# One decoder layer on one core: sample-state loads issued behind the weights, the prompt read in eight pieces, the first layer norm's output kept as the second residual

## The chip, the cores and the metric

The kernel runs on one core of a Trainium2 chip. The metric is the device time of one execution, in microseconds (us). A core has a matrix engine (PE, with its weight loads listed apart as PEld), a vector engine (DVE), a scalar engine (ACT), a general engine (POOL) and a synchronisation engine (SP); each takes its own instructions strictly in their order. Loads and stores are DMAs: SP, ACT or POOL issues one, 16 DMA engines carry it out, and a semaphore tells when it has landed.

## The reference

One layer for two groups of requests that share all weights: 256 prompt tokens and 8 sample tokens (one for each of 8 requests), model width 2048. Cut to what matters here:

```
proj = x @ w_in                      # 16400 columns: q, k, v, g, a, conv inputs, memory query, gates z_a, z_b, z_m
A: gated linear attention            # per head a 256 x 512 state; S_new = decay * S + k^T v
B: short gated convolution
M: cross-attention into 256 memory tokens
merged = sig(z_a)*y_a + sig(z_b)*y_b + sig(z_m)*y_m
x  = LayerNorm(alpha * x + merged @ w_o)                    # first layer norm
f  = (silu(dwconv3(x @ w_gate)) * (x @ w_up)) @ w_down
x  = LayerNorm(alpha * x + f)                               # second residual: the first norm's output
```

The prompt starts from zero states. Each of the 8 samples brings its own memory keys and values (`cache_mem_k`, `cache_mem_v`, 256 rows each) and, for each of 4 heads, its own state of 256 x 512 numbers (`state_gla`), and the new states are outputs. All arrays are fp32.

## The kernel before

**Matrix products.** All 264 tokens (256 prompt, 8 sample) stand as columns; a weight matrix is streamed once, in *granules* of two k-tiles by 512 columns (512 KB). A granule is loaded by one DMA that SP issues (`ws`, four buffers), rounded to a high part by ACT (`wh`, three buffers) and its remainder is formed by DVE (`wl`, three buffers), lines 238 to 257. PE then runs three products for each of its 8 tiles: wh with the activations' high part, wh with their low part, wl with the high part (lines 279 to 281), so 24 matmuls of 264 columns for a granule. Some 650 granules follow each other: w_in's groups, the memory weights, w_o, then for the feed-forward part a first pass over 24 of 43 column tiles of gate and up with its share of w_down, and a second pass over the other 19. A `group` is 512 output columns: eight granules for a depth of 2048.

**What shares the queues.** Between the granules the samples' work is threaded in as *units*: 16 for the memory keys, 16 for the values, 32 that read a state (`sum_unit`) and, in the feed-forward part, 32 that update it (`update_unit`, lines 778 to 792). An update unit loads a state tile `S` (512 KB, line 782) and a row of v, copied to all partitions (`T<-dv`, 256 KB, line 784); ACT scales the two halves of S (line 790), DVE adds k times v to each (line 791), and two granules later in program order SP issues the store (line 792). The tiles S have three buffers (tag `S4`), so the load for one unit waits for the store of the unit three before it. Units are put in a list (`queue`); `tick`, called once a granule, pops one when `clock[1]` granules have passed (6 in the feed-forward part) and at least three granules of the group are left, and `ahead` traces the loads of the next ones. The program is then ordered by a list scheduler: program order gives the priority, `high_priority(offset)` moves a piece earlier (granule loads by 700 places, casts by 450), and where an instruction's buffer is free in the scheduler's reckoning it may be put ahead of older ones on its engine. `tc.issue_after(i)` adds an edge: instructions traced inside it stand behind instruction i on their engine, without a wait.

**The start.** The prompt x (256 x 2048) comes in four pieces of 512 columns, two DMAs of 256 KB each (`load_x`, line 73); the samples' rows `xs` come by SP. PE keeps busy with nine products of constants (`keep_warm(9)`, line 99), each recorded as two passes, transposes x tile by tile (line 305, 128 x 128) into PSUM, and `split` (line 289) makes the high part XH on ACT and the low part XL on DVE. `turn_start` (line 308) does the samples and the first four k-tiles; `turn_x`, called from the first group's granules, loads the other pieces and transposes two k-tiles a granule.

**The residuals.** `residual` (line 1008) adds a high and a low part on POOL into a tile of tag `T4` (16 buffers). It is called four times on XH, XL for the first layer norm and four times on X1H, X1L, the split output of the first norm, for the second (line 1120). The normalised tile itself (`r`, line 1073) is split and then released.

Of the kernel before, what the change touches and what calls it, by code (L numbers as in the profile page):

```python
# [9 lines left out]
F32 = mybir.dt.float32  # L10
# [7 lines left out]
P = 128  # L18
NP = 256
# [15 lines left out]
def layer_kernel(ctx, tc, x_prompt, x_sample, mem_prompt, cache_mem_k, cache_mem_v, state_gla, state_conv,  # L35
# [3 lines left out]
    nc = tc.nc  # L39
# [11 lines left out]
    def big(dt=F32, shape=(P, 4, NT)):  # L51
        return sb.tile(list(shape), dt, tag="T4", bufs=16, name=nm("T4"))
# [17 lines left out]
    xc = []  # L70
    xs = t2(F32, (P, P))

    def load_x(c):
        t = big(F32, (P, 2, 512))
        for m in range(2):
            (nc.sync if m or c else S).dma_start(t[:, m], x_prompt[0, m * P:(m + 1) * P, c * 512:(c + 1) * 512])
        xc.append(t)

    load_x(0)
    nc.sync.dma_start(xs, x_sample.rearrange("b l (k f) -> (b l k) f", f=P))  # L80

# [16 lines left out]

    keep_warm(9)
    LEVELS = (1, 2, 4, 8, 16, 32, 64)  # L100
# [59 lines left out]
    queue = []  # L160
    loaded = [0]
    clock = [0, 4]
# [6 lines left out]
    def ahead(n):  # L169
        k = 0  # L170
        for it in queue:
            if it[0] is not None:
                it[2] = it[0]()
                it[0] = None
            if it[2] is not None:
                k += 1
            if k >= n:
                break
# [59 lines left out]
    def granule(srcs, n, ncols):  # L238

        lead[0] += 1  # L240
        with tc.high_priority(offset=0 if lead[0] <= 8 else 700):
            st = sb.tile([P, n, ncols], F32, tag="ws", bufs=4, name=nm("ws"))
            for a, o in srcs:
                c = a.shape[-1]
                nc.sync.dma_start(st[:, :, o:o + c], a.rearrange("(k p) c -> p k c", p=P))
        with tc.high_priority(offset=0 if lead[0] <= 8 else 450):
            wh = sb.tile([P, n, ncols], F32R, tag="wh", bufs=3, name=nm("wh"))
            wl = sb.tile([P, n, ncols], F32R, tag="wl", bufs=3, name=nm("wl"))
            with ExitStack() as after:
                if lead[0] == 1:  # L250
                    S.copy(wh, st)
                for i in first.pop(0) if first else []:
                    after.enter_context(tc.issue_after(i))
                if lead[0] > 1:
                    S.copy(wh, st)  # L255
                V.tensor_sub(wl, st, wh.bitcast(F32))  # L256
        return wh, wl
# [36 lines left out]
    def turn_x(g, n):  # L294
        if g in (0, 2, 4):
            load_x(len(xc))
        if g + 4 <= 16 and g:
            for kt in range(g + 2, g + 4):
                with tc.high_priority(offset=60):
                    turn_x1(kt)  # L300

    def turn_x1(kt):
        pt = small()
        for m in range(2):
            T.transpose(pt[:, m * P:(m + 1) * P], xc[kt // 4][:, m, kt % 4 * P:(kt % 4 + 1) * P], ident)
        return split(XH[:, kt, 0:NP], XL[:, kt, 0:NP], pt[:, 0:NP])

    def turn_start():
        pt = small()
        T.transpose(pt[:, 0:P], xs, ident)  # L310
        i = split(XH[:, :, NP:NT], XL[:, :, NP:NT], pt[:, 0:P].rearrange("p (b k) -> p k b", b=NS))
        first.append(i + turn_x1(0))
        first.append(turn_x1(1))
        turn_x1(2)
        turn_x1(3)

# [12 lines left out]
    for c in range(2):  # L329
        pm = group([(win, MQ0 + c * 512, 512)], 16, xh, xl, before=None if c else turn_x)  # L330
        t = big()
# [759 lines left out]
    for t0, t1 in ((0, 24), (24, 43)):  # L1091
# [26 lines left out]
        for c in range(4):  # L1118
            if t0 == 0:
                r2.append(residual(c, X1H, X1L))  # L1120
            elif c == 0:
# [114 lines left out]
```

## Time and profile before

| | |
|---|---|
| time, median of 3 runs | 2073.56 us (2070.11 to 2074.78) |
| profiled execution | 2072.68 us, span 2070.7 us |
| mean granted clock of PE | 0.992 |
| PE busy | 2015.7 us (97%) |
| DVE, ACT, POOL busy | 1273.2, 1012.3, 197.1 us |
| DMA | 439.96 MB, mean 212 GB/s |

The profile is that of one execution. A row of a time line or of a group gives start, duration, engine, line and operation, with output<-input; in brackets stands how long the engine had been idle before and what released it. A row of stretches gives the busy time of each engine, with the number of instructions in parentheses, then the clock that PE was granted (1.00 is full, 0.50 half), the DMA engines' mean busy share and GB/s.

### The profile page before, as it was taken

The page shows a single profiled execution, that of the slowest core. Times are in us where ns is not written, and L with a number is a line of the kernel's source. Part 1 is how long each engine was busy: PE and PEld are TensorE (multiplying, and loading weights), DVE is VectorE, ACT ScalarE, POOL GpSimd, SP SyncE. Part 2 cuts the span into 40 slices and gives each one's busy share as a digit, 9 for nine tenths or more (in the row PEclk, how much of TensorE's full clock was granted, in tenths as well). Part 3 has the DMA queues.
Part 4 walks back from the last instruction along what each step waited for, and adds up shares of the span by engine and source line. Part 5 has one row for each costly group of instructions (what it writes and reads, how often), then busy time and mean ns, then how long its engine had stood idle before and what let it go on. Part 6 is the DMA issues. An engine that isn't in the chain of part 4 may idle for free.

```text
span 2070.7 us, 38389 instructions
## 1 busy us (share of the span) xinstructions
PE 2015.7 (97%) x15762; PEld 1965.8 (95%) x15762; DVE 1273.2 (61%) x1902; ACT 1012.3 (49%) x1399; POOL 197.1 (10%) x249
## 2 busy tenths in 40 slices
PE   8999999999999999999999999999899999999996
PEld 8888999999999999999999997988899999999996
DVE  4666585758596755455445769666565445555546
ACT  4433564657474554345444447555454334444432
POOL 4000031303130010100001004000000000000001
PEclk9999999999999999999999999999999999999998
DMA  8796776666577685666565567988896566665753
GB/s 283 237 318 196 230 218 200 210 194 215 179 216 215 197 224 174 180 183 181 179 180 177 177 200 272 312 293 272 296 298 208 179 183 178 180 183 166 234 176 102
DMA packets 233487, 439.96 MB, mean 212 GB/s; under 512 B 22665, under 2 KB 27230, under 8 KB 233048
## 3 DMA queue, kind: packets, MB, share of 16 engines
q1 hardware_dynamic: 227152, 425.42, 66.6%
q0 software_dynamic: 5440, 10.79, 1.6%
q8 instruction: 123, 2.02, 0.4%
q10 hardware_dynamic: 720, 1.31, 0.2%
q14 instruction: 52, 0.43, 0.1%
HBM read 410.76 MB, written 26.85 MB: 211 GB/s over the span
## 4 chain that ended last, share of the span: by engine, by line
PE 60%; DMA 6%; DVE 4%; ACT 1%; issue 1%; SPq 0%; DVEq 0%; ACTq 0%
PE mm L279 19%; PE mm L280 19%; PE mm L281 19%; DMA S<-in_state_gla_dram 5%; DVE wl L256 2%; DMA out_dram<-S 1%; PE sm L725 1%; ACT wh L255 1%; DVE S L791 1%; ACT S L790 0%; DMA T<-dv 0%; PE acc L413 0%; PE acc L414 0%; DVE YT L1195 0%; DVE YT L1201 0%
## 5 line engine op out<-in xcount | busy, mean ns | idle before, releaser
L256 DVE TENSOR_TENSOR wl<-ws,wh 128x1024 fp32r<-128x1024 f32 (+1 forms) x650 | 801.2, 1236 | 587.3 <-ACT wh L255 585.0
L255 ACT CAST wh<-ws 128x1024 fp32r<-128x1024 f32 (+1 forms) x649 | 672.2, 1039 | 794.2 <-PE mm L280 676.4
L279 PE MATMUL mm<-XH,wh 128*128 128x264 f32 (+1 forms) x2064 | 593.1, 287 | 0.2 <-ACT T L814 0.2
L281 PE MATMUL mm<-XH,wl 128*128 128x264 f32 (+1 forms) x2064 | 589.0, 285 | 0.0
L280 PE MATMUL mm<-XL,wh 128*128 128x264 f32 (+1 forms) x2064 | 588.7, 285 | 0.0
L279 PE MATMUL mm<-T,wh 128*128 128x264 f32 x1456 | 415.2, 285 | 0.6 <-ACT G L843 0.6
L281 PE MATMUL mm<-T,wl 128*128 128x264 f32 x1456 | 414.2, 284 | 0.0
L280 PE MATMUL mm<-T,wh 128*128 128x264 f32 x1456 | 414.0, 284 | 0.0
L281 PE MATMUL mm<-X1H,wl 128*128 128x264 f32 x1376 | 394.6, 287 | 13.1 <-DVE wl L256 13.1
L279 PE MATMUL mm<-X1H,wh 128*128 128x264 f32 x1376 | 395.8, 288 | 10.0 <-DVE G L1110 4.6
L280 PE MATMUL mm<-X1L,wh 128*128 128x264 f32 x1376 | 393.1, 286 | 0.5 <-DVE X1L L289 0.5
L279 PEld LDWEIGHTS mm<-XH,wh 128*128 128x128 f32 (+1 forms) x2064 | 389.8, 189 | 2.9 <-ACT T L814 0.4
L280 PEld LDWEIGHTS mm<-XL,wh 128*128 128x128 f32 (+1 forms) x2064 | 389.1, 189 | 2.4
L281 PEld LDWEIGHTS mm<-XH,wl 128*128 128x128 f32 (+1 forms) x2064 | 388.2, 188 | 0.3
L281 PEld LDWEIGHTS mm<-X1H,wl 128*128 128x128 f32 x1376 | 260.4, 189 | 16.5 <-DVE wl L256 16.5
L279 PEld LDWEIGHTS mm<-T,wh 128*128 128x128 f32 x1456 | 274.1, 188 | 1.1 <-ACT G L843 1.1
L279 PEld LDWEIGHTS mm<-X1H,wh 128*128 128x128 f32 x1376 | 261.4, 190 | 13.7 <-DVE G L1110 5.7
L280 PEld LDWEIGHTS mm<-T,wh 128*128 128x128 f32 x1456 | 274.1, 188 | 0.0
L281 PEld LDWEIGHTS mm<-T,wl 128*128 128x128 f32 x1456 | 273.8, 188 | 0.0
L280 PEld LDWEIGHTS mm<-X1L,wh 128*128 128x128 f32 x1376 | 261.1, 190 | 1.2 <-DVE X1L L289 0.7
L791 DVE SCALAR_TENSOR_TENSOR S<-T,qks,S 128x512 f32<-128x512 f32 x64 | 52.9, 851 | 71.0 <-ACT S L790 58.8
L790 ACT ACTIVATE S<-S,eas 128x512 f32<-128x512 f32 x64 | 44.0, 717 | 95.6 <-DMA S<-in_state_gla_dram 95.6
(347 smaller groups left out, 1524.9 us busy)
## 6 DMA issues: line engine op xcount, KB each, us to landing
ws<-in_w_in_dram SPq DMA_DIRECT2D x256, 512.0 KB, 3.7
ws<-in_w_ffn_down_dram SPq DMA_DIRECT2D x84, 512.0 KB, 4.4
ws<-in_w_ffn_gate_dram SPq DMA_DIRECT2D x80, 512.0 KB, 4.3
ws<-in_w_ffn_up_dram SPq DMA_DIRECT2D x80, 512.0 KB, 4.8
S<-in_state_gla_dram SPq DMA_DIRECT2D x64, 512.0 KB, 5.2
ws<-in_w_gla_out_dram SPq DMA_DIRECT2D x32, 512.0 KB, 3.7
ws<-in_w_o_dram SPq DMA_DIRECT2D x32, 512.0 KB, 4.0
out_dram<-S SPq DMA_DIRECT2D x32, 512.0 KB, 7.0
```

Source lines behind the costliest of these rows:

```text
L255: S.copy(wh, st)
L256: V.tensor_sub(wl, st, wh.bitcast(F32))
L279: T.matmul(p, wh[:, t, cs], xh(kt), start=(kt == 0), stop=False)
L280: T.matmul(p, wh[:, t, cs], xl(kt), start=False, stop=False)
L281: T.matmul(p, wl[:, t, cs], xh(kt), start=False, stop=(kt == nk - 1))
L725: T.matmul(pt, kd[:, st, kt * P:(kt + 1) * P], vt[:, st], start=(st == 0), stop=(st == 1))
L790: S.activation(sg[:, kt], sg[:, kt], AF.Copy, scale=eas[:, h, kt, b:b + 1])
L791: V.scalar_tensor_tensor(sg[:, kt], pb, qks[:, 1, h, kt, b:b + 1], sg[:, kt], ALU.mult, ALU.add)
```

## The change

Three edits, and what goes with them.

1. **Loads behind the weights.** `granule` notes its DMA in `staged`; `ahead` traces every unit's loads inside `tc.issue_after(staged[0])`, so that on SP they stand behind the granule last traced.
2. **x in eight pieces.** `load_x` takes 256 columns, two DMAs of 128 KB, 16 in all. The first group's first granule is a single k-tile (g0=1, 256 KB), so that the group has nine granules. Each piece is turned by four transposes into one PSUM tile and one `split` of 512 columns. Through `first`, a granule's cast and remainder are put behind the split of the piece that the granule before it called for. `xs` is loaded by ACT's queue, and `keep_warm` runs 12 products.
3. **Second residual.** `r2` takes the normalised tiles `rs[c]` themselves; the four POOL additions on X1H, X1L go.

```diff
     def load_x(c):
-        t = big(F32, (P, 2, 512))
+        if c % 2 == 0:
+            xc.append(big(F32, (P, 2, 512)))
         for m in range(2):
-            (nc.sync if m or c else S).dma_start(t[:, m], x_prompt[0, m * P:(m + 1) * P, c * 512:(c + 1) * 512])
-        xc.append(t)
+            (nc.sync if m or c else S).dma_start(xc[c // 2][:, m, c % 2 * 256:c % 2 * 256 + 256],
+                                                 x_prompt[0, m * P:(m + 1) * P, c * 256:(c + 1) * 256])
     load_x(0)
-    nc.sync.dma_start(xs, x_sample.rearrange("b l (k f) -> (b l k) f", f=P))
+    S.dma_start(xs, x_sample.rearrange("b l (k f) -> (b l k) f", f=P))
...
-    keep_warm(9)
+    keep_warm(12)
...
         for it in queue:
             if it[0] is not None:
-                it[2] = it[0]()
+                with ExitStack() as behind:
+                    if staged:
+                        behind.enter_context(tc.issue_after(staged[0]))
+                    it[2] = it[0]()
                 it[0] = None
...
-                nc.sync.dma_start(st[:, :, o:o + c], a.rearrange("(k p) c -> p k c", p=P))
+                staged[:] = [nc.sync.dma_start(st[:, :, o:o + c], a.rearrange("(k p) c -> p k c", p=P)).ins]
...
             with ExitStack() as after:
-                if lead[0] == 1:
-                    S.copy(wh, st)
                 for i in first.pop(0) if first else []:
                     after.enter_context(tc.issue_after(i))
-                if lead[0] > 1:
-                    S.copy(wh, st)
+                S.copy(wh, st)
                 V.tensor_sub(wl, st, wh.bitcast(F32))
...
     def turn_x(g, n):
-        if g in (0, 2, 4):
-            load_x(len(xc))
-        if g + 4 <= 16 and g:
-            for kt in range(g + 2, g + 4):
-                with tc.high_priority(offset=60):
-                    turn_x1(kt)
+        c = (g + 1) // 2 + 1
+        if c < 8:
+            load_x(c)
+            with tc.high_priority(offset=60):
+                first.append(turn_x2(c))
+    def turn_x2(c):
+        pt = small()
+        for a in range(2):
+            for m in range(2):
+                T.transpose(pt[:, (2 * a + m) * P:(2 * a + m + 1) * P],
+                            xc[c // 2][:, m, (c % 2 * 2 + a) * P:(c % 2 * 2 + a + 1) * P], ident)
+        return split(XH[:, 2 * c:2 * c + 2, 0:NP], XL[:, 2 * c:2 * c + 2, 0:NP], pt.rearrange("p (a t) -> p a t", a=2))
     def turn_start():
+        first.append(turn_x2(0))
         pt = small()
         T.transpose(pt[:, 0:P], xs, ident)
         i = split(XH[:, :, NP:NT], XL[:, :, NP:NT], pt[:, 0:P].rearrange("p (b k) -> p k b", b=NS))
-        first.append(i + turn_x1(0))
-        first.append(turn_x1(1))
-        turn_x1(2)
-        turn_x1(3)
+        first[0] = first[0] + i
...
-        pm = group([(win, MQ0 + c * 512, 512)], 16, xh, xl, before=None if c else turn_x)
+        pm = group([(win, MQ0 + c * 512, 512)], 16, xh, xl, before=None if c else turn_x, g0=1 - c)
...
             if t0 == 0:
-                r2.append(residual(c, X1H, X1L))
+                r2.append(rs[c])
```

How the instructions move is seen in the order in which they stand on an engine. First SP in the feed-forward part's first pass, at a gate group and the up group behind it; `ws` is a granule, `S` a unit's state, `T<-dv` its row of v, `out_dram<-S` its store. Before:

```order
L245 DMA ws_16039<-in_w_ffn_gate_dram 128x2x512
L792 DMA out_dram<-S_2381_17086 128x2x512
L245 DMA ws_16069<-in_w_ffn_gate_dram 128x2x512
L784 DMA T_2455_17710<-dv 128x512
L782 DMA S_2454_17708<-in_state_gla_dram 128x2x512
L245 DMA ws_16100<-in_w_ffn_gate_dram 128x2x512
L245 DMA ws_16130<-in_w_ffn_gate_dram 128x2x512
L792 DMA out_dram<-S_2410_17339 128x2x512
L245 DMA ws_16194<-in_w_ffn_up_dram 128x2x512
L784 DMA T_2489_17999<-dv 128x512
L782 DMA S_2488_17997<-in_state_gla_dram 128x2x512
L245 DMA ws_16224<-in_w_ffn_up_dram 128x2x512
```

And now:

```order
L784 DMA S_2249_15998<-in_state_gla_dram 128x2x512
L250 DMA ws_16002<-in_w_ffn_gate_dram 128x2x512
L786 DMA T_2250_16000<-dv 128x512
L250 DMA ws_16032<-in_w_ffn_gate_dram 128x2x512
L250 DMA ws_16063<-in_w_ffn_gate_dram 128x2x512
L250 DMA ws_16093<-in_w_ffn_gate_dram 128x2x512
L794 DMA out_dram<-S_2249_15998 128x2x512
L250 DMA ws_16123<-in_w_ffn_gate_dram 128x2x512
L250 DMA ws_16187<-in_w_ffn_up_dram 128x2x512
L784 DMA S_2275_16221<-in_state_gla_dram 128x2x512
L250 DMA ws_16225<-in_w_ffn_up_dram 128x2x512
L786 DMA T_2276_16223<-dv 128x512
```

Before, a unit came every three granules, and a state's load stood one granule behind the store of the unit three before it, whose buffer it takes. Now a unit comes every six granules on average, its own store is issued before the next unit's load, and the buffer that a load takes was stored from some 13 to 15 granules ago. Counted over the whole order, the loads of the 32 update units stood behind granules 392 to 474 and now stand behind 393 to 557 (the first seven still behind 393 to 407); the ACT work on a state stands about two granules ahead of the granule behind which its load is issued, in both.

Second, SP at the start of the program, before (`T` is a piece of x or, 128x128, the samples' rows):

```order
L76 DMA T_2_64<-in_x_prompt_dram 128x512
L80 DMA T_1_63<-in_x_sample_dram 128x128
L245 DMA ws_128<-in_w_in_dram 128x2x512
L76 DMA T_15_134<-in_x_prompt_dram 128x512 x2
L245 DMA ws_161<-in_w_in_dram 128x2x512
L76 DMA T_19_167<-in_x_prompt_dram 128x512 x2
L245 DMA ws_204<-in_w_in_dram 128x2x512
```

And now:

```order
L78 DMA T_2_64<-in_x_prompt_dram 128x256 x2
L250 DMA ws_118<-in_w_in_dram 128x512
L78 DMA T_2_64<-in_x_prompt_dram 128x256
L250 DMA ws_145<-in_w_in_dram 128x2x512
L78 DMA T_16_151<-in_x_prompt_dram 128x256 x3
L250 DMA ws_185<-in_w_in_dram 128x2x512
L78 DMA T_16_151<-in_x_prompt_dram 128x256
L250 DMA ws_224<-in_w_in_dram 128x2x512
L78 DMA T_25_230<-in_x_prompt_dram 128x256 x4
```

Half as much x and half as much weight now stand ahead of the first product, and the fourth granule's weights stand ahead of the fifth piece of x (the first two of the four DMAs into T_25).

Third, PE at the start (`sm<-ident,T` are transposes of x or, 128x128 alone ahead of them, of the samples). Before:

```order
L310 MATMUL sm_98<-ident,T_1_63 128x128
L305 MATMUL sm_102<-ident,T_2_64 128x128 x2
L305 MATMUL sm_107<-ident,T_2_64 128x128 x2
L279 MATMUL mm_124<-XH,wh_130 128x264
L279 MATMUL mm_125<-XH,wh_130 128x264
L305 MATMUL sm_112<-ident,T_2_64 128x128 x2
L280 MATMUL mm_124<-XL,wh_130 128x264
```

And now, from the first transpose and, in the second fence, at the end of the first granule (wh_120, wl_121) and the beginning of the second (wh_147):

```order
L308 MATMUL sm_101<-ident,T_2_64 128x128 x4
L315 MATMUL sm_108<-ident,T_1_63 128x128
L281 MATMUL mm_114<-XH,wh_120 128x264
L308 MATMUL sm_126<-ident,T_2_64 128x128 x4
L308 MATMUL sm_154<-ident,T_16_151 128x128 x4
L282 MATMUL mm_114<-XL,wh_120 128x264
```

```order
L308 MATMUL sm_193<-ident,T_16_151 128x128 x4
L281 MATMUL mm_117<-XH,wh_120 128x264
L282 MATMUL mm_117<-XL,wh_120 128x264
L308 MATMUL sm_233<-ident,T_25_230 128x128 x4
L283 MATMUL mm_117<-XH,wl_121 128x264
L281 MATMUL mm_114<-XH,wh_147 128x264
```

T_2 holds pieces 0 and 1, T_16 pieces 2 and 3, T_25 pieces 4 and 5. Before, the transposes within the first granule's first half were those of the first of four pieces; now the transposes of five of eight pieces, twenty and the samples' one, stand ahead of the first granule's twelfth and last matmul.

More of the change, by code (lines that the diff above doesn't have):

```diff
@@ L160, in layer_kernel @@
     queue = []
-    loaded = [0]
+    staged = []
     clock = [0, 4]
@@ L294, in turn_x @@
     def turn_x(g, n):
-        if g in (0, 2, 4):
-            load_x(len(xc))
-        if g + 4 <= 16 and g:
-            for kt in range(g + 2, g + 4):
-                with tc.high_priority(offset=60):
-                    turn_x1(kt)
-    def turn_x1(kt):
-        pt = small()
-        for m in range(2):
-            T.transpose(pt[:, m * P:(m + 1) * P], xc[kt // 4][:, m, kt % 4 * P:(kt % 4 + 1) * P], ident)
-        return split(XH[:, kt, 0:NP], XL[:, kt, 0:NP], pt[:, 0:NP])
+        c = (g + 1) // 2 + 1
[4 more added lines that the diff above has]
+    def turn_x2(c):
+        pt = small()
+        for a in range(2):
[3 more added lines that the diff above has]
+        return split(XH[:, 2 * c:2 * c + 2, 0:NP], XL[:, 2 * c:2 * c + 2, 0:NP], pt.rearrange("p (a t) -> p a t", a=2))
     def turn_start():
+        first.append(turn_x2(0))
         pt = small()
```

## The prediction

> **What bounds the kernel now.** I read the page's totals first, then the busy time by stretches, then the waits inside the stretch that loses most, then the chain that ended last.
>
> ```profile
> span 2070.7 us, 38389 instructions
> PE 2015.7 (97%) x15762; PEld 1965.8 (95%) x15762; DVE 1273.2 (61%) x1902; ACT 1012.3 (49%) x1399; POOL 197.1 (10%) x249
> ```
>
> PE is the bound: no edit here takes a matmul of 264 columns away, so only its lost time can be won. The stretches say where that lies (columns: PE, PEld, DVE, ACT, POOL, granted clock, DMA share, GB/s).
>
> ```profile
> 1.00:8.00 7.00, 4.59 (x21) 4.23 (x21) 0.56 (x6) 2.68 (x5) 6.07 (x14) 1.00 0.83 234
> 8.70:12.00 3.30, 3.30 (x17) 3.27 (x16) 1.50 (x3) 0.98 (x2) 2.22 (x7) 0.50 1.05 383
> 15.50:18.80 3.30, 2.85 (x13) 2.86 (x14) 2.19 (x4) 1.57 (x3) 3.30 (x10) 0.50 0.92 310
> 1281.90:1285.10 3.20, 2.82 (x13) 2.83 (x14) 3.20 (x3) 1.61 (x4) 2.80 (x1) 0.50 0.81 253
> 1418.40:1421.70 3.30, 3.30 (x14) 3.21 (x15) 3.30 (x6) 2.55 (x6) 0.00 (x0) 0.50 0.60 179
> 1462.80:1466.00 3.20, 3.20 (x16) 3.20 (x16) 1.58 (x2) 0.00 (x0) 0.00 (x0) 0.50 0.87 248
> 1277.00:1553.00 276.00, 252.49 (x1971) 245.54 (x1971) 182.15 (x277) 151.30 (x227) 6.02 (x3) 0.98 0.88 288
> 1560.00:2050.00 490.00, 490.00 (x4030) 489.90 (x4029) 256.02 (x352) 207.29 (x259) 4.93 (x4) 1.00 0.60 180
> 2050.00:2070.70 20.70, 2.87 (x19) 2.04 (x17) 16.53 (x31) 3.70 (x8) 8.46 (x6) 0.66 0.28 105
> ```
>
> From 1560 to 2050 PE never idles and starts a matmul every 490 / 4029 = 0.1216 us; a granule of 24 is then 2.92 us. From 1277 to 1553 it starts only 1971 in 276 us, which at that rate take 239.7: **36.3 us are lost** there, 23.5 as idle time (276 - 252.5), 5.1 in three stretches of about 3.4 us at half clock (half of each), the rest as late weight loads. This stretch holds all 32 state updates. The first 20 us and the tail of 20 us are the other losses; the tail's code is untouched. Who waits in the lossy stretch (line, what it waited for, us in total, times, longest):
>
> ```profile
> ACT S L790 <- DMA S<-in_state_gla_dram: 95.6, 27, 6.3
> DVE S L791 <- ACT S L790: 58.8, 16, 5.4
> DVE wl L256 <- ACT wh L255: 17.9, 14, 5.6
> PE mm L281 <- DVE wl L256: 13.1, 16, 3.2
> PE mm L279 <- DVE G L1110: 4.6, 4, 2.5
> ```
>
> Read from below: PE waits for the weights' remainder or for a bank that DVE empties, DVE for ACT, and ACT stands 95.6 us on 27 states that have not landed, with the casts of later granules queued behind. The chain shows why a state is late:
>
> ```profile
> 1403.10 7.22 DMA out_dram<-S
> 1410.33 6.06 DMA S<-in_state_gla_dram
> 1416.48 0.73 ACT S L790
> ...
> 1417.90 0.42 DVE G L1110
> ```
>
> The load starts the moment a store has landed: the tile's buffer is the stored one. Landing times in this crowd (count, KB, us):
>
> ```profile
> out_dram<-S SPq DMA_DIRECT2D x28, 512.0 KB, 7.1
> S<-in_state_gla_dram SPq DMA_DIRECT2D x27, 512.0 KB, 5.6
> T<-dv SPq DMA_DIRECT2D x19, 256.0 KB, 7.3
> ```
>
> A store and the load behind it need 7.1 + 5.6 = 12.7 us, against three granules (8.8 us) from one unit to the next.
>
> **The loads behind the weights.** SP's order now has a unit every six granules, 17.5 us, and the buffer was stored from 13 granules (38 us) earlier, so the 7.1 falls out. The state still lands close to its use. Let PE begin granule k-6 at 0. ACT can cast granule j when PE has finished j-3, and the costs are these:
>
> ```profile
> L256 DVE TENSOR_TENSOR wl<-ws,wh 128x1024 fp32r<-128x1024 f32 (+1 forms) x650 | 801.2, 1236 | 587.3 <-ACT wh L255 585.0
> L255 ACT CAST wh<-ws 128x1024 fp32r<-128x1024 f32 (+1 forms) x649 | 672.2, 1039 | 794.2 <-PE mm L280 676.4 <-PE mm L472 45.9 <-issue 38.6
> L790 ACT ACTIVATE S<-S,eas x58: 706/719/727, 1293.4 to 1543.9; 128x512 f32<-128x512 f32 x58
> ```
>
> Granule k's DMA waits for the buffer of k-4, free when its remainder is done at 1.04 + 1.24 = 2.3. The state's load follows it at about 2.9 and lands at 8.5. ACT has cast k-2 by 5.8 + 1.0 = 6.9 (PE began k-4 at 5.8), stands 1.6 us, scales both halves (2 x 0.72) by 9.9, casts k-1 by 11.0, and DVE has its remainder at 12.2; PE wants it at 14.8, the start of k-1. The row of v is issued behind granule k+1 (5.7) and lands at 13.0 at the crowd's 7.3; the one addition that mostly stands ahead of that remainder then ends at 13.7 and the remainder at 15.0: 0.2 late at worst. So an isolated unit costs PE about nothing, and the next has 17.5 us to come. The kernel has one such unit already, a state loaded behind granule 220 and used behind the cast of 218:
>
> ```profile
> 741.13 0.72 ACT L738 ACTIVATE T<-S,qas 128x512 f32<-128x512 f32 x1 [0.82 <-DMA S<-in_state_gla_dram]
> 720.00:750.00 30.00, 30.00 (x245) 29.83 (x244) 20.68 (x28) 19.76 (x28) 5.78 (x3) 1.00 0.75 212
> ```
>
> ACT stands 0.82 us and PE is busy for all 30. What does not spread are the first seven units (granules 393 to 407). Bounds for the 36.3: all won, or only the part of edit 3 below. I take 1.0 us of loss for each of those seven (derived in edit 3) and none for the other 25. The same edge lies on the loads of keys, values and state sums; counted over the order, six of those 64 now stand as close as the unit above, against three; I take 0, bounds -1 to +3 (six times half of ACT's 0.82, rounded up).
>
> **The residual kept.** Four POOL additions go.
>
> ```profile
> 1261.39 18.75 POOL L1010 TENSOR_TENSOR T<-X1H,X1L 128x1056 f32<-128x1056 f32 x3
> 1272.01 5.84 DVE L791 SCALAR_TENSOR_TENSOR S<-T,qks,S 128x512 f32<-128x512 f32 x2
> 1277.78 3.43 DVE L256 TENSOR_TENSOR wl<-ws,wh 128x1024 fp32r<-128x1024 f32 x1
> L791 DVE SCALAR_TENSOR_TENSOR S<-T,qks,S x63: 740/747/2957, 1274.9 to 1548.9; 128x512 f32<-128x512 f32 x63
> ```
>
> Beside them two additions on DVE take 5.84 us where 1.5 is normal, and a remainder 3.43 instead of 1.24: 6.5 us on DVE, out of which come PE's longest wait of the list above (3.2, at 1278) and the half clock at 1281.9 (1.7 us), 4.9 in all. That leaves 36.3 - 4.9 = 31.4 for 32 units, 1.0 each, the price used above. The kept tiles need no room: four of them and twelve of a pass's activations fill T4's sixteen buffers, as the four new tiles did. So edits 1 and 3 together: 36.3 - 7 x 1.0 = **29.3 won**.
>
> **The start.**
>
> ```profile
> 1.12 4.21 PE L97 MATMUL warm<-ones 128*128 128x128 f32 x18 [1.12 <-DVE ones L86]
> 8.38 0.50 PE L305 MATMUL sm<-ident,T 128*128 128x128 f32 x2 [2.67 <-DVE XL L289]
> 14.12 1.04 ACT L255 CAST wh<-ws 128x1024 fp32r<-128x1024 f32 x1 [1.40 <-DMA ws<-in_w_in_dram]
> 0.00:18.87 18.87, 4.00 (x10) 2.83 (x10) 0.82 0.89 293
> 0.00:18.87 18.87, 3.28 (x13) 1.90 (x14) 0.82 0.89 293
> L782 SPq DMA_DIRECT2D S<-in_state_gla_dram x29: 367/421/663, 1287.4 to 1538.6; - x29
> ```
>
> Before, by 18.87, where the second half-clock stretch ends, PE has done some 30 products (the fourth row counts the 10 of line 279; there are three such lines) and 14 of 33 transposes (the 13 of line 305 in the fifth row, and the samples'). Now the warm products end at 1.12 + 24 x 0.234 = 6.7 instead of 5.3, the first product comes at about 8.7 as before, but PE then has 12 products and 21 transposes (0.50 for two with their tails; 0.2 us each taken) ahead of the second granule, and waits for piece 4. Ahead of that piece's end stand 1.25 MB of x, 1.75 MB of weights and 64 KB, as many bytes as stood ahead of the end of the third granule's weights before, cast at 14.12; by the GB/s of the stretches they are through at 12.3 (1.6 MB by 8.0, then 0.37 to 0.4 MB a us). From 12.3: transposes to 13.1, then up to 18.87 eight more transposes (1.6) and 34 products: 46 products and 29 transposes, 16 x 0.12 + 15 x 0.2 = 4.9 us ahead. From 14.1 with one half-clock stretch: 24 and 29, 2.3 us ahead. Other end, a loss: eight more issues by SP at 0.42 us (the median of the last row) put 3.4 us on the weights. I take **3 us won**.
>
> At one place a rule bears on this. The clock is halved behind an idle time of only 1.88 us:
>
> ```profile
> 1462.16 0.39 PE L281 MATMUL mm<-X1H,wl 128*128 128x264 f32 x1 [1.88 <-DVE wl L256]
> ```
>
> The Trainium skill, "TensorE: Matmul & The Clock Gate", section "What's actually happening", has the clock fall after an idle window of about 3.4 us. By that rule none of the three half-clock stretches would be owed to these waits, 5.1 us less would be won, and the time would be 2046; the trace disagrees, with 0.50 behind an idle time of 1.88 us, and the trace decides.
>
> **The sum.** 2072.7 (the profiled execution) - 29.3 - 3 = 2040.4; the median of the runs lies 0.9 above that execution: **2041**.
>
> **The rivals.** (a) *The price is the unit's, not the crowd's*: every state is still loaded about two granules behind its use. For it: ACT will stand on most states. Against: the unit at 741. Then 31.4 stay, and 2072.7 - 4.9 - 3 + 0.9 = 2066. (b) *Sixteen issues are dearer than eight* and the start loses 3.4 instead of winning 3: 2047. For it, eight more issues lie in SP's strict order ahead of weights; against, its loads of x land while weights are moving, at a DMA share of 0.83 and over. The Trainium skill, "DMA: Bandwidth & Descriptors", section "Measured (HBM→SBUF, 128 partitions, SWDGE, issued from GpSimd)", asks for 1 MiB a DMA and over; its fit in "Anatomy of one DMA", 2.0 us and bytes at 436 GB/s, estimates 16 x 2.3 against 8 x 2.6 us, 16 us more and 2054 if they ran one after the other. The trace does not show them one after the other. (c) *Slower*: the state's load, its row and its store now stand between granules in SP's strict order, one set every six over 165 granules instead of 82; if the store waits for DVE, and DVE for the row, the weights behind are late each time. At the longest wait a unit shows now, 2.5 us, 32 x 2.5 = 80 against 36.3: 2073 + 44 - 3 = 2114. It decides from 36.3 / 32 = 1.1 us a unit. Against it, by the steps above the store is ready at 13.7 + 0.7 = 14.4, 3 us behind its place (k+4, 3.9 granules after k, 11.4), and a granule's DMA, issued at 2.3 for a cast at 11.7, has 9.4 - 5.6 = 3.8 us in hand at a state's landing time. (d) *It does not do what it says*, because what waits is the shared DMA: 2073. Against: the bytes are the same, over twice the time.
>
> **How the numbers follow.** Forecast 0.70 (its own range 2032 to 2050: residue 0 to 13 us, start from 4.9 won to nothing); (a) 0.13; (b) 0.09; (c) 0.04; (d) 0.04. 2031 to 2058 holds the forecast, (b) and the part of (a) in which up to two thirds of the price stay (2055): about 0.8. A measurement tells 0.2%, 4.1 us, from no change. Faster: forecast, (b) and nearly all of (a), 0.90; the same: (d) and the rest of (a), 0.05; slower 0.05.
>
> **What would show it.** Right: the updates spread over some 480 us from 1250 on; ACT's wait for states still there, about 1.5 us each, but PE's wait for remainders under 5 us; no half clock behind 1300; DVE's additions near 0.75 us throughout; the first product near 8.7 and no idle PE behind 15 us. Wrong: PE idle at each unit (a), SP late with `ws` behind a store (c), PE idle over 3 us before the second granule (b).

## The result, and the profile after

The changed kernel takes **2038.97 us** (median; 2038.18 to 2039.97) against 2074.17 us of the kernel before in the same comparison: a ratio of 0.9834, 95% interval 0.9817 to 0.9851, so 34.4 us less (30.9 to 38.0). The prediction was 2041. The profiled execution took 2038.21 us, 34.5 less than the one before.

The page's totals, after:

```profile
span 2036.5 us, 38343 instructions
PE 2004.7 (98%) x15768; PEld 1958.3 (96%) x15768; DVE 1262.9 (62%) x1895; ACT 1008.3 (50%) x1390; POOL 175.7 (9%) x245
```

PE is still the bound, and its products are the same. The stretches, after (PE, PEld, DVE, ACT, POOL, granted clock, DMA share, GB/s):

```profile
8.70:12.00 3.30, 2.11 (x17) 1.71 (x14) 2.81 (x4) 3.19 (x5) 3.30 (x7) 1.00 1.06 384
15.50:18.80 3.30, 3.30 (x30) 3.30 (x29) 1.92 (x2) 1.58 (x3) 3.30 (x16) 1.00 1.05 371
1246.00:1310.00 64.00, 63.91 (x484) 60.03 (x485) 52.80 (x105) 50.24 (x87) 2.20 (x3) 1.00 0.92 301
1277.00:1553.00 276.00, 274.30 (x2234) 272.13 (x2233) 174.59 (x274) 151.37 (x219) 0.00 (x0) 1.00 0.80 261
1310.00:1553.00 243.00, 241.30 (x1963) 239.13 (x1962) 151.18 (x234) 129.25 (x187) 0.00 (x0) 1.00 0.77 254
1560.00:2010.00 450.00, 449.61 (x3687) 448.33 (x3686) 248.77 (x348) 205.85 (x264) 4.93 (x4) 1.00 0.68 215
```

From 1277 to 1553 PE now starts 2233 weight loads where it started 1971. At 0.1216 us each that is 271.5 of 276 us: 4.5 us are lost in place of 36.3. The clock is 1.00 in every row. Where the work on the states went (the first three rows, of the whole execution; before, 58 of the 64 scalings lay between 1277 and 1553), who waits between 1277 and 1553 (the fourth), and PE's wait for remainders from 1240 to 1780 (the last):

```profile
L784 SPq DMA_DIRECT2D S<-in_state_gla_dram x32: 368/463/1281, 1245.8 to 1741.6; - x32
L792 ACT ACTIVATE S<-S,eas 128x512 f32<-128x512 f32 x64 | 43.4, 716 | 71.2 <-DMA S<-in_state_gla_dram 67.2
L793 DVE SCALAR_TENSOR_TENSOR S<-T,qks,S 128x512 f32<-128x512 f32 x64 | 46.8, 747 | 64.4 <-DMA T<-dv 64.3
ACT wh L257 <- PE mm L282: 63.1, 41, 1.9
PE mm L283 <- DVE wl L258: 1.1, 2, 0.8
```

The loads lie over 496 us instead of some 290, and the slowest of DVE's additions takes 754 ns, where one took 2957. ACT still waits for states (67.2 us) and DVE for rows of v (64.3 us), but PE's wait for remainders is 1.1 us where it was 13.1. What is new is the fourth row: 41 times ACT waits for PE to give a buffer back, that is, the casts run ahead of PE. Before, that happened seven times there:

```profile
ACT wh L255 <- PE mm L280: 8.3, 7, 2.3
```

The start, after (PE's time line; idle time and its releaser in brackets):

```profile
1.12 4.54 PE L99 MATMUL warm<-ones 128*128 128x128 f32 x24 [1.12 <-DVE ones L88]
5.50 0.60 PE L308 MATMUL sm<-ident,T 128*128 128x128 f32 x4
7.46 0.39 PE L281 MATMUL mm<-XH,wh 128*128 128x264 f32 x1 [1.25 <-ACT wh L257]
13.27 0.70 PE L308 MATMUL sm<-ident,T 128*128 128x128 f32 x4 [1.56 <-DMA T<-in_x_prompt_dram]
```

The first product comes at 7.46 instead of 8.58, and behind 13.27 PE no longer idles. The 2.67 us that PE idled ahead of 8.38 in the kernel before were not a wait for x: the samples' transpose and those of the first k-tile were done by 5.71 and held both PSUM buffers of tag `sm`, until ACT and DVE had split them. ACT's time line there, two rows before and one after:

```profile
6.79 1.04 ACT L251 CAST wh<-ws 128x1024 fp32r<-128x1024 f32 x1 [4.07 <-DMA ws<-in_w_in_dram]
7.75 0.53 ACT L289 CAST XH<-sm 128x128 fp32r<-128x128 f32 x2
6.14 0.76 ACT L291 CAST XH<-sm 128x512 fp32r<-128x512 f32 x2 [2.92 <-PE sm L308]
```

Before, ACT stood in order 4.07 us for the first granule's weights, cast them, and split only then. Now the cast stands behind the split, and one buffer takes four transposes.

### The profile page after: what moved, and what is told of

It reads as the page before. It is cut to its first block, busy times and chain, and to the rows that moved or that the text cites. A ratio compares the mean times of both kernels' runs of the same rounds, so it can differ in the third digit from the quotient of the medians.

```text
span 2036.5 us, 38343 instructions
## 1 busy us (share of the span) xinstructions
PE 2004.7 (98%) x15768; PEld 1958.3 (96%) x15768; DVE 1262.9 (62%) x1895; ACT 1008.3 (50%) x1390; POOL 175.7 (9%) x245
## 5 line engine op out<-in xcount | busy, mean ns | idle before, releaser
L258 DVE TENSOR_TENSOR wl<-ws,wh 128x1024 fp32r<-128x1024 f32 (+2 forms) x651 | 799.7, 1231 | 578.5 <-ACT wh L257 576.8
L257 ACT CAST wh<-ws 128x1024 fp32r<-128x1024 f32 (+2 forms) x651 | 674.3, 1038 | 776.8 <-PE mm L282 656.7
L793 DVE SCALAR_TENSOR_TENSOR S<-T,qks,S 128x512 f32<-128x512 f32 x64 | 46.8, 747 | 64.4 <-DMA T<-dv 64.3
L792 ACT ACTIVATE S<-S,eas 128x512 f32<-128x512 f32 x64 | 43.4, 716 | 71.2 <-DMA S<-in_state_gla_dram 67.2
```

Of the source, the lines that this page charges most:

```text
L792: S.activation(sg[:, kt], sg[:, kt], AF.Copy, scale=eas[:, h, kt, b:b + 1])
L793: V.scalar_tensor_tensor(sg[:, kt], pb, qks[:, 1, h, kt, b:b + 1], sg[:, kt], ALU.mult, ALU.add)
```

## The experiments

Times are medians; each ratio is to the kernel before, run beside it on the same chip. 0.1216 us is PE's pace, used to turn counted starts into time.

### Each edit alone

**Edit 1 alone**, in the kernel before:

```diff
-                it[2] = it[0]()
+                with ExitStack() as behind:
+                    if staged:
+                        behind.enter_context(tc.issue_after(staged[0]))
+                    it[2] = it[0]()
```

> The kernel before with edit 1 alone (unit loads behind the weights; units every six granules). Theory (a unit with six granules to itself costs PE nothing, one in the crowd 1.0 us): of 36.3 us the 4.9 of the POOL additions and at most 7 of the first seven units stay, 24 to 31 us won, 2043 to 2049; no half clock between 1300 and 1553 except near the POOL additions. Rival (a), the price is the unit's: about 2073, with PE idle at each of the 32 units.

2049.43 us, ratio 0.9894 (0.9876 to 0.9911): 22.0 us less (18.4 to 25.7), just outside the range that was expected; one stretch at half clock, from 1344 on, was not expected either. The stretches, and what is left at their beginning (DVE's time line):

```profile
1246.00:1310.00 64.00, 59.84 (x406) 53.21 (x406) 56.31 (x95) 45.39 (x80) 23.83 (x7) 0.95 0.78 258
1310.00:1553.00 243.00, 237.91 (x1927) 236.13 (x1926) 150.31 (x236) 128.36 (x187) 0.00 (x0) 0.99 0.78 249
1271.32 5.84 DVE L794 SCALAR_TENSOR_TENSOR S<-T,qks,S 128x512 f32<-128x512 f32 x2
```

Behind 1310 it is nearly the changed kernel (1926 starts against 1962). Ahead of 1310, beside POOL's additions, 406 starts stand against 485: 9.6 us, and DVE's two additions take 5.84 us as before.

**Edit 3 alone**, in the kernel before:

```diff
-                r2.append(residual(c, X1H, X1L))
+                r2.append(rs[c])
```

> The kernel before with edit 3 alone (the four POOL additions gone). Theory: the 3.2 us wait and 1.7 us of half clock at 1278 go, 4.9 us won, 2068.7. Rival: the ring of three state buffers (a store of 7.1 and a load of 5.6 us in three granules of 8.8) sets the pace of the units anyway, and what is won at 1278 is waited for later: 0 to 1 us won, 2073.

2065.01 us, ratio 0.9965 (0.9952 to 0.9979): 7.3 us less (4.4 to 10.0). The additions on DVE at the same place, and the two stretches:

```profile
1270.27 1.40 DVE L791 SCALAR_TENSOR_TENSOR S<-T,qks,S 128x512 f32<-128x512 f32 x2
1246.00:1310.00 64.00, 63.13 (x464) 57.64 (x463) 52.39 (x103) 47.15 (x85) 2.19 (x3) 1.00 0.93 325
1310.00:1553.00 243.00, 224.76 (x1757) 220.31 (x1756) 155.79 (x243) 135.20 (x203) 0.00 (x0) 0.97 0.89 291
```

1.40 us in place of 5.84, with POOL not at work beside them. The kernel before has these two stretches so:

```profile
1246.00:1310.00 64.00, 57.64 (x388) 50.21 (x387) 55.13 (x93) 44.89 (x80) 23.82 (x7) 0.97 0.82 287
1310.00:1553.00 243.00, 225.19 (x1770) 219.52 (x1770) 155.38 (x240) 133.28 (x201) 0.00 (x0) 0.99 0.90 294
```

The 76 starts gained ahead of 1310 (9.2 us) are the whole gain; 14 are lost behind it (1.7 us), which leaves 7.5. So the rival, that what is won here is waited for later, holds for a sixth of it.

**Edit 2 alone**: the changed kernel with the two edits above undone.

> The kernel before with edit 2 alone (x in eight pieces, twelve warm products). Theory: 3 to 4 us won, 2069.5 to 2070.5, and by 18.87 us some 51 products of 264 columns done against 29 before; the feed-forward stretch loses what it lost, 36 us. Rival (b), sixteen issues are dearer: 2077.

2068.42 us, ratio 0.9979 (0.9969 to 0.9990): 4.4 us less (2.1 to 6.4); sixteen issues cost nothing that shows. By 18.87 (lines 278 and 305, the first of the three product lines, and the transposes):

```profile
0.00:18.87 18.87, 4.94 (x17) 3.20 (x18) 1.00 0.92 309
0.00:18.87 18.87, 4.15 (x24) 2.80 (x24) 1.00 0.92 309
```

The three product lines start 17 each, 51 in all, where they started 29; and 25 transposes are done (the samples' one included) against 14. 22 products are 2.7 us; eleven transposes at 0.15 to 0.2 are another 1.7 to 2.2: 4.4 to 4.9. The clock is 1.00 where it was 0.82.

Added up, 22.0 + 7.3 + 4.4 = 33.7 of 34.4: the three edits hardly touch one another.

### Is it the place behind the weights, or the distance?

The changed kernel, edge kept, with units closer together:

```diff
-    clock[1] = 6
+    clock[1] = 3
```

> The changed kernel with a unit every three granules instead of six in the feed-forward part; the edge that puts loads behind weights is kept, as are edits 2 and 3. Theory (the spacing takes the price away): the 25 units behind the first seven cost 0.8 to 1.0 us each again, 20 to 25 us, 2059 to 2064, with ACT waiting on states that start when a store lands. Rival (the place behind the weights takes it away, not the distance): 2039.

2060.55 us, ratio 0.9948 (0.9934 to 0.9961): 21.6 us of the gain are gone (23.6 by the two ratios), which is all of edit 1. The place in SP's queue by itself is worth nothing; the distance of six granules is what pays.

```profile
1310.00:1553.00 243.00, 227.61 (x1807) 223.61 (x1806) 152.69 (x239) 131.37 (x196) 0.00 (x0) 0.99 0.88 290
S<-in_state_gla_dram SPq DMA_DIRECT2D x28, 512.0 KB, 6.9
```

### Is it the store that a load waits for?

That was the prediction's cause: 7.1 us of a store and 5.6 of a load in a ring of three buffers. In the kernel before, the stores were given another source, so that a state's buffer is free when DVE is done with it:

```diff
-            later(2, lambda: nc.sync.dma_start(o_sgla[0, b, h].rearrange("(k p) v -> p k v", p=P), sg))
+            held = X1H.rearrange("p k t -> p (k t)")[:, 0:1024].rearrange("p (k v) -> p k v", k=2).bitcast(F32)
+            later(2, lambda: nc.sync.dma_start(o_sgla[0, b, h].rearrange("(k p) v -> p k v", p=P), held))
```

> The kernel before with the 32 stores of the update units reading the first norm's output instead of the unit's state tile (the new states that it writes are therefore not the reference's; bytes, places in program order and the work on ACT and DVE are the same). A state's load then waits for DVE's addition three units earlier and no longer for the store of it. Theory (the ring store-load, 12.7 us in three granules of 8.8, is the price of 31.4 us): 20 to 31 us won, 2042 to 2053. Rival (the DMA crowd itself, units on top of weights, is the price): within 4 us of the kernel before, 2069 to 2073. A price in between says how much of it is either's.

2073.45 us, ratio 1.0002 (0.9992 to 1.0011): nothing. The stores are out of the loads' way, and ACT waits for the states all the same:

```profile
ACT S L790 <- DMA S<-in_state_gla_dram: 85.8, 25, 6.7
1277.00:1553.00 276.00, 252.16 (x1968) 246.33 (x1968) 182.81 (x274) 151.65 (x227) 8.36 (x3) 0.98 0.89 289
```

1968 starts against 1971. The same edit in the changed kernel with a unit every three granules:

> The changed kernel with a unit every three granules, as in the run before of that spacing (2060.6), and the stores reading the first norm's output, so that no load waits for a store (the new states are again not the reference's). Theory (the distance helps because the store falls out of the load's path): most of the 21.6 us that the close spacing cost goes, 2039 to 2046. Rival (the crowd): 2058 to 2062.

2062.38 us, ratio 0.9954 (0.9939 to 0.9968), against 0.9948 with the stores in the way. Twice no difference: **the ring of store and load is not the price.** In the prediction's chain the store did end last at some units; with it gone, ACT stands on the states nearly as long. Nor is the price a wait of SP at a store that DVE has not finished: in these two kernels the stores do not wait for DVE's additions.

### Is it the crowd on the DMA engines, or the engines that stand in order?

All three of the next kernels have a unit every three granules and leave a part of it out. First, all loads and stores, but no work:

```diff
-            for kt in range(2):
-                S.activation(sg[:, kt], sg[:, kt], AF.Copy, scale=eas[:, h, kt, b:b + 1])
-                V.scalar_tensor_tensor(sg[:, kt], pb, qks[:, 1, h, kt, b:b + 1], sg[:, kt], ALU.mult, ALU.add)
```

> The changed kernel with a unit every three granules and with the update units' ACT and DVE work left out; their loads and stores stay at their places, every three granules (the new states written are the old ones). Theory A (the price of the close spacing is that ACT and DVE, which cast the weights, stand in order on tiles that have not landed): 2037 to 2043, with the DMA share between 1277 and 1553 still near 0.89. Theory B (the DMA engines are too full and weights land late): 2055 to 2062.

2032.55 us, ratio 0.9812 (0.9799 to 0.9826), below what theory A expected and below the changed kernel.

```profile
1246.00:1310.00 64.00, 63.71 (x482) 59.84 (x483) 45.18 (x92) 42.38 (x73) 2.19 (x3) 1.00 0.99 351
1277.00:1553.00 276.00, 276.00 (x2271) 276.00 (x2271) 157.01 (x243) 133.76 (x188) 0.00 (x0) 1.00 0.92 312
1310.00:1553.00 243.00, 243.00 (x2000) 243.00 (x1999) 137.21 (x209) 115.93 (x163) 0.00 (x0) 1.00 0.91 308
1560.00:2010.00 450.00, 450.00 (x3701) 449.91 (x3701) 235.58 (x329) 191.49 (x241) 4.92 (x4) 1.00 0.59 179
```

At a DMA share of 0.92 and 312 GB/s, more than any other kernel moved there, PE never idles from 1277 on. A full set of DMA engines alone costs nothing.

Second, all work, but no store:

```diff
-            later(2, lambda: nc.sync.dma_start(o_sgla[0, b, h].rearrange("(k p) v -> p k v", p=P), sg))
```

> The changed kernel with a unit every three granules and the update units' stores left out (the new states are not written): 512 of a unit's 1280 KB fewer. Theory A: ACT and DVE wait as before for S and its row, 2052 to 2062, less by what earlier landings give. Theory B: the DMA share falls from 0.89 to about 0.8, the share of the changed kernel, and the time to 2039 to 2045.

2044.22 us, ratio 0.9872 (0.9852 to 0.9892). Landing times of states between 1277 and 1553, in this kernel, then in the one without work and in the changed kernel:

```profile
S<-in_state_gla_dram SPq DMA_DIRECT2D x26, 512.0 KB, 5.4
S<-in_state_gla_dram SPq DMA_DIRECT2D x26, 512.0 KB, 6.0
S<-in_state_gla_dram SPq DMA_DIRECT2D x17, 512.0 KB, 6.6
```

Three quarters of the 21.6 us go (two thirds by the ratios), as theory B (the crowd) had it, although B alone fell with the run before. So the DMAs cost nothing by themselves, and the stores among them cost 16 us where ACT and DVE work on the states. A reading that fits both is that the landing counts where an engine stands in order behind it, and that it is shorter here, 5.4 us against 6.9 with the stores. It is not shown: the kernel before had 5.6 us and the full price, and the landing does not follow the DMA share (6.0 us at 0.92 without the work, 6.6 at 0.80 in the changed kernel). Weights land earlier too without the stores (3.7 us in the median, against 5.7 and 6.9 for the two kinds with them), and no run here separates the two.

Third, the same work on tiles that are there already:

```diff
-            nc.sync.dma_start(sg, state_gla[0, b, h].rearrange("(k p) v -> p k v", p=P))
...
-                S.activation(sg[:, kt], sg[:, kt], AF.Copy, scale=eas[:, h, kt, b:b + 1])
-                V.scalar_tensor_tensor(sg[:, kt], pb, qks[:, 1, h, kt, b:b + 1], sg[:, kt], ALU.mult, ALU.add)
+                S.activation(sg[:, kt], flat[:, 512 * kt:512 * kt + 512], AF.Copy, scale=eas[:, h, kt, b:b + 1])
+                V.scalar_tensor_tensor(sg[:, kt], flat[:, 1024:1536], qks[:, 1, h, kt, b:b + 1], sg[:, kt], ALU.mult, ALU.add)
```

(`flat` is the first norm's output.)

> The changed kernel with clock three, states not loaded, ACT's and DVE's work of each unit done on the first norm's output instead of the state and its row, the rows loaded but not read, the stores kept (the new states are not the reference's). The same instructions stand on ACT and DVE, a unit every 1.3 granules or so, and none waits for a load. Theory A (the waits, not the work): 2037 to 2045. Rival C (the work itself, 1.43 us on ACT and 1.49 on DVE a unit, takes the engines from the casts): 2055 or more.

2045.27 us, ratio 0.9871 (0.9858 to 0.9885), just above what theory A allowed. That is 12.7 us above the kernel without work, where three granules with loads cost 28.0. So the work, packed about twice as densely, costs less than work that waits for loads does; what it still loses lies mostly between 1300 and 1400, where 29.2 us of ACT's waits for stores lie, since with no load between them the units follow each other faster than the three buffers are stored (all between 1277 and 1553):

```profile
ACT S L792 <- DMA out_dram<-S: 35.6, 18, 4.4
```

So this run bounds the work's own price from above, no more.

### How far apart is enough?

```diff
-    clock[1] = 6
+    clock[1] = 4
```

> The changed kernel with a unit every four granules (11.7 us) instead of six (17.5). Theory A: a wait of a state costs PE only what has not been caught up before the next one, so most of the 21.6 us that three granules cost is gone at four: 2040 to 2048. Theory B (crowd): the loss goes with the bytes per time, 16 us or so of it left, 2052 to 2057.

**2065.31 us**, ratio 0.9970 (0.9959 to 0.9981): slower than with three granules, and outside of what either theory expected. The chain of waits in this kernel suggests why; between 1403 and 1518 it goes round in a loop from one unit's load to the next, of which this is one turn (start, us, what):

```profile
1466.68 0.37 SPq L250
...
1467.10 6.45 DMA S<-in_state_gla_dram
...
1474.20 0.71 ACT S L792
1474.91 0.95 ACT wh L257
...
1477.03 1.41 DVE S L793 x2
1478.44 1.15 DVE wl L258
...
1479.60 0.37 SPq L250
...
1480.02 6.23 DMA S<-in_state_gla_dram
```

SP issues a granule's weights (line 250) when DVE has made the remainder of the granule four before; the unit's state is behind them in SP's order and lands 6.45 us later; ACT scales it and only then casts the next granule; DVE adds and makes the remainder; that frees the buffer for which SP's next weights wait, and the next state stands behind those. This turn took 12.92 us (1466.68 to 1479.60) without a step of PE in it; in other turns the chain passes through PE as well. The mean turn, from the loads of ten units:

```profile
L784 SPq DMA_DIRECT2D S<-in_state_gla_dram x10: 506/638/1644, 1403.3 to 1518.3; - x10
```

(1518.3 - 1403.3) / 9 = **12.8 us a turn**. PE needs 4 x 24 x 0.1216 = 11.7 for four granules: 1.1 us are lost at each unit, 28 us for the 25 behind the first seven, and 26.3 were measured (2065.3 - 2039.0; 28.2 by the two ratios). This agreement says that the loss is spread over the units; it would come out so for any cause that holds each of them up. For the loop as the cause there is the chain alone: no run here shortens a step of it. At six granules, 17.5 us, such a turn has 4.7 us to spare; the 41 times that ACT waits for PE there are a sign of it. With three granules (8.8 us) the loop does not set the pace: the difference to 12.8 would be 4.0 us a unit, and 21.6 / 25 = 0.9 was paid. Two states are under way at once there, the units are not evenly spaced, and the chain changes between states, rows and stores; this price is measured, but I have not worked it out from a turn.

### The start again

> The changed kernel with the transposes of a piece of x moved only 30 places ahead instead of 60, so that those of the fifth piece stand behind the first eight products of the second granule and not ahead of the first granule's last product. Theory: of the 1.56 us that PE waits for that piece at most 1 us is won, about 2038, not told from 2039 by the times; the trace of the first 20 us shows that wait shorter. Rival: the remainders and casts that stand behind the piece's split come later and PE waits there instead, 2039 to 2041.

The edit is `offset=60` to `offset=30` around the transposes that `turn_x` calls. 2035.24 us (2035.01 to 2035.75), ratio 0.9820 (0.9807 to 0.9832). The start:

```profile
12.99 0.30 PE L308 MATMUL sm<-ident,T 128*128 128x128 f32 x1 [0.45 <-DVE wl L258]
```

Ahead of the fifth piece's transposes PE idles 0.45 us, put down to DVE's remainder, where it idled 1.56 for the piece's DMA, and by 18.87 PE has done 61 products where the changed kernel has 49: 1.5 us. Its four times lie below the four of the changed kernel, but they come from another chip, and the intervals of the two ratios overlap: a further gain is likely, not shown.

> The changed kernel with 9 warm products instead of 12. Theory (the half clock of 8.7 to 12.0 came from the idle time behind the warm products): the warm passes end at 4.5, transposes start at 5.5 as they do now, and no half clock follows, since the idle time is 1 us; then the twelve products won nothing. Rival: the clock falls to 0.50 for one stretch of about 3.4 us behind the first product, 1.7 us lost, and the twelve products are what won half of the start's gain.

2038.50 us in a single run, and no half clock in the start.

```profile
1.12 4.21 PE L99 MATMUL warm<-ones 128*128 128x128 f32 x18 [1.12 <-DVE ones L88]
5.12 0.71 PE L308 MATMUL sm<-ident,T 128*128 128x128 f32 x4
```

The three more warm products win nothing that this shows. The first product comes at 7.19, and PE's longest idle time in the start is 1.38 us. So it was not these products that took the half clock away; the 2.67 us of idle time that stood ahead of it in the kernel before are gone with nine of them too. That this is owed to ACT's split, which no longer stands behind the first cast, is read from the time lines; no run undoes it alone.

## Why the prediction was right, and where it was not

The time was 2 us off, and each term lies inside the interval that was measured for it:

| term | predicted | measured alone |
|---|---|---|
| loads behind the weights | 24.4 (36.3 - 4.9 - 7) | 22.0 (18.4 to 25.7) |
| residual kept | 4.9 | 7.3 (4.4 to 10.0) |
| start | 3 | 4.4 (2.1 to 6.4) |

**What bounds the kernel, and how much is lost there**: right. 36.3 us by the count of starts between 1277 and 1553 became 4.5. (The stretch held not all of the updates' work but nearly all, 58 of 64 scalings.)

**Why a state is late**: wrong. The prediction read the chain at 1403, store 7.22 and load 6.06 one behind the other, and set 7.1 + 5.6 = 12.7 us against the 8.8 of three granules; "the 7.1 falls out" was to be the gain. Two runs that took the store out of the load's way won nothing (1.0002, and 0.9954 against 0.9948). That a crowd of units costs nothing once a store no longer delays a load is the step that fell. It did not spoil the forecast, because the crowd's price was measured, and the 24.4 us rest on the list for an isolated unit, six granules from the next, whatever made the crowd dear. The 12.7 is close to the 12.8 us of a turn at four granules by accident: in the chain there a turn is landing, scaling, cast, additions, remainder and SP's next issue. The prediction had each of these steps in its list for an isolated unit, but did not close the list to a loop by asking what the next unit's load waits for. What exactly costs the time at three granules stays open; the runs there show that more than half of it (28.0 - 12.7 of 28.0 us) takes ACT's and DVE's work on the states and the loads together.

**An isolated unit costs PE about nothing, and six granules isolate it**: right, for the reason given there, that the next unit is 17.5 us away. In detail it was too kind: ACT stands 2.6 us a state (67.2 for 26) where 1.6 was worked out, and DVE 3.2 us a row (64.3 for 20). PE hardly sees it (1.1 us of waits for remainders), because the casts have run ahead of PE by then (the 41 waits on PE). Two small sums in that list are off, and neither decides: five granules of 2.92 us end at 14.6, not 14.8, so the remainder at 15.0 would be 0.4 late at worst; and the store's place, 11.4 us behind k's issue at 2.3, is 13.7, so the store, ready at 14.4, is 0.7 behind it and not 3.

**The residue of 7 us on the first seven units**: right in size, wrong in place. Against the kernel without the units' work (three granules) the changed one has 37 starts fewer between 1310 and 1553 (1962 against 1999) and 15 fewer behind 1560 (3686 against 3701), 52 x 0.1216 = 6.3 us; between 1246 and 1310, where the first seven loads lie, it has none fewer (485 against 483); from 1277 to 1310 it starts 2233 - 1962 = 271 in 33 us, which is PE's full pace. So all units cost 0.2 us each on the mean, and the first seven, closer together, nothing. The step that fell is the carrying over of the crowd's mean price, 1.0, to seven units that begin it; why these cost nothing was not tried.

**The residual**: right in mechanism, DVE's additions fall from 5.84 to 1.40 us for two. It was sized by the longest wait and one half clock, 4.9; the count of starts ahead of 1310 gives 9.2 gained there and 1.7 given back behind.

**The start**: right in sum. The wait for piece 4 ended at 13.27, inside 12.3 to 14.1, and by 18.87 51 products and 25 transposes were done with edit 2 alone, where 46 and 29 had been worked out for the early end of that wait. "The first product comes at about 8.7 as before" was wrong: 7.46, and 7.19 with nine warm products, so the warm products only put it off. In the kernel before, ACT's split stood behind the cast of a whole granule; the split now stands first, and the cast ahead of the first product is that of half a granule, 256 KB. In rival (b), the 2054 is a slip: 16 us more on 2041 are 2057.

**The half clock**: the 5.1 us were won back; in the changed kernel no stretch at 0.50 is left ahead of the tail. The 2046 that the prediction worked out by the rule of the Trainium skill, "TensorE: Matmul & The Clock Gate", section "What's actually happening", did not come.

**The rivals**: (a), the price is the unit's, would have been 2066: it fell, a unit costs 0.2 us at six granules. (b) fell with edit 2 alone. (c), SP late behind a store that waits for DVE, did not come at six granules, yet it was the nearest to the chain at four granules, a loop through SP's order, where 1.1 us a unit are lost. (d), the shared DMA, fell with the time; and the run that kept the DMAs and left out the work shows that they cost nothing alone.

## What to carry to other kernels

When loads are threaded into a stream that in-order engines work off, close the loop before counting a wait: from one unit's issue over landing, the in-order work and the freed buffer to the next unit's issue. Here a distance well above the turn (17.5 us against 12.8) made the price all but vanish, and at three granules neither a free buffer nor a better place in the queue helped. The turn is no general price list: at four granules the units paid the difference, at three, where it was larger, less. A chain of waits names what ended last, not what would win time if it were gone: that takes a run with the suspect removed and the rest kept. The store was such a suspect and fell; the loop at four granules has not had its run.

## What the runs showed of the hardware

Full DMA engines were no price by themselves: 312 GB/s at a share of 0.92 beside PE at full pace cost nothing. A 512 KB state landed in 5.4 us (units without stores) to 6.9 us (with them) at three granules, but not by the share: 6.0 us at 0.92, and 6.6 at 0.80 in the changed kernel.

Idle times of nearly one length ended differently for the clock. Two in the kernel with four granules (PE's time line, then the stretch behind each):

```profile
1339.23 0.39 PE L283 MATMUL mm<-X1H,wl 128*128 128x264 f32 x1 [1.88 <-DVE wl L258]
1567.42 0.52 PE L281 MATMUL mm<-T,wh 128*128 128x264 f32 x1 [1.90 <-ACT wh L257]
```

```profile
1339.30:1342.70 3.40, 3.40 (x28) 3.40 (x29) 2.81 (x3) 0.00 (x0) 0.00 (x0) 1.00 0.67 190
1567.60:1570.90 3.30, 2.78 (x12) 2.48 (x13) 3.30 (x4) 1.66 (x2) 0.00 (x0) 0.50 0.32 93
```

Behind 1.88 us PE went on at 1.00, behind 1.90 at 0.50. The reason lies in where the idle time falls. The half-clock stretches begin on a grid of 3.413 us: those of the kernel before, at 1281.9, 1418.4 and 1462.8, are 136.5 and 44.4 us apart, 40 and 13 such steps. Counted back from the stretch at 1567.5, a grid line lies at 1338.8: it cuts the first idle time into 1.5 and 0.4 us, while the second lies whole in one step. Over nine of the kernels here, behind the first 20 us, all 23 steps at full clock in which PE idled 1.84 us or more were followed by a step at 0.50, none with 1.48 or less was, and of the seven between 1.59 and 1.73 four were. So half a step of idle time costs half of the next one, 1.7 us. A step that is itself at half clock needs less: the four with 0.52 to 1.27 us of idle time were followed by another at 0.50, the 27 with 0.51 or less by one at 1.00. The Trainium skill, "TensorE: Matmul & The Clock Gate", section "What's actually happening", has a free-running window of 4096 cycles, about 3.4 us: the grid agrees with it, 3.413 us. Its idle window as a whole as the condition does not agree: about half of one was enough.
